# Layer 1's heads: three row blocks of the first head come early into the unused third pair of split weights, gated rows leave from the normed tile

## The chip, the core and the metric

The kernel runs on one core of one Trainium2 chip. The core has five engines that run at the same time, each through its own list of instructions in order: PE (matrix products; PEld is its weight load), DVE and ACT (elementwise work), POOL (here small elementwise work and the issue of some DMAs) and SP (the issue of most DMAs). An instruction waits at the head of its engine's list until the semaphores it needs are set, and everything behind it on that engine waits with it. The metric is the device time of one launch in microseconds (us); lower is better.

## The reference, cut to what matters

Two layers work on a prompt of 512 tokens and on 8 running streams of 16 new tokens, 640 rows together, with a width of 2048. Layer 0 is an attention layer and is not touched here. Layer 1 is gated linear attention with 4 heads, keys of 256 and values of 512 per head:

```python
def gla_chunk(S, inp):
    q, k, v, g = inp
    b = jnp.cumsum(g, axis=1)
    ...
    o = jnp.einsum('bhcs,bshe->bche', a, v) + jnp.einsum('bchd,bhde->bche', q_in, S)
    S = jnp.exp(b_last)[..., None] * S + jnp.einsum('bshd,bshe->bhde', k * jnp.exp(b_last[:, None] - b), v)
    return S, o

def gla_mixer(h, w_in, w_a2, b_a, g_out, w_out, S0=None):
    ...
    q, k, v, r, a_lr = jnp.split(h @ w_in, [nk, 2 * nk, 2 * nk + nv, 2 * nk + 2 * nv], axis=-1)
    ...
    o = o * lax.rsqrt(jnp.mean(o * o, axis=-1, keepdims=True) + EPS) * g_out...
    y = (o.reshape(B, T, nv) * jax.nn.silu(r.astype(f32))) @ w_out
```

So each head's output rows are normed, multiplied by a gate, and then go through the output weights w_out (2048 by 2048). In the trunk the product is gated again, added to the residual, and normed once more.

## The kernel before, in words

**Precision.** Every large product is made of three products of rounded halves. A helper `halves(hi, lo, x)` (L133) copies x into hi on ACT (L134) and puts x minus hi into lo on DVE (L135). `split` (L139) does so for a raw weight tile of 128 by 1024. It takes one of two pairs of tiles (tags wh and wl in the pool wp), and every third time, where `ring3["pool"]` is set, a third pair in another pool. Raw weights come through two tiles (tag wr).

**Order.** PE's list is written out by hand. As the code writes it, it keeps a clock of its own, `pe["now"]` (L50), to which each product adds its estimated time (L54 to L63: a product of 512 columns adds 512/2400 + 0.0133). The main work is a generator that is driven step by step. After each step `Side.tick` (L316) looks at the lanes, which are generators of side work, and lets those run whose due time on this clock has come; `side.after(wait, what)` (L288) puts a call at a time. `side.until(condition)` (L335) does side work only: where nothing is due it moves the clock by 0.2 and tries again. Waits written in the code (`yield step(5.0)`) are thus places in PE's list and not times on the chip. The lists of the other four engines are ordered by a scheduler that looks ahead over the whole program.

**The stage.** In the last part of layer 1, the main work is first `plain` (L629): 24 pieces of q and k weights, each with 48 products of 320 columns (L651). Pieces 22 and 23 make the last 128 columns; piece 22 reads the tiles in the slots 16 to 31 of `hp`, piece 23 those in the slots 0 to 15. Then come two calls of `share` (L683): share g multiplies head g's four row blocks of gated output (each 128 by 640) by the head's rows of w_out, in four column stretches c and five token blocks a. One step of it is three products of 512 columns (L697) for one row block, and the first token block goes through the row blocks 0, 1, 2, 3 in turn.

**Side work in this stage.** `decays` (L1601) makes q and k of a head ready. `prompt_lane` (L1662) goes through 16 units (head, chunk of 128 tokens). For each it makes the output `o`, norms it into a tile `on` (two buffers, L1567 to L1576), and one unit later calls `leave` (L1589): four transposes of `on` on PE (L1593), the product with the gate tile on DVE, written over the gate tile (L1594), and a DMA on POOL's queue that takes the gate tile to a DRAM tensor `og_d` (L1595). The next gate tile is fetched by `fetch_gate`, also on POOL's queue (L1580). `sample_lane` (L1791) does the same for the running streams. For each head it takes 32 state tiles of 128 by 512 (tag s0, seven buffers, S0 = 7 on L34; numbers below count them over all heads), in groups of four: `ask` (L1775) loads one, a product reads it (L1855), PE and DVE update it (L1861, L1863), and `leaves` (L1786) stores it to the output 1.0 later on the clock and asks for another one 7.0 after that. With seven buffers, state n + 7 can only be asked for when state n has left. All these loads and stores are on POOL's queue. The product of L1855 may be put into the list in the very step in which its last state is asked for.

**Row blocks.** The lane `fetches` (L1878) brings back the row blocks from `og_d` through two tiles (tag pl), which `plain` also uses for its results (L1504), and splits each into two slots of `hp`. It starts with block 0 when half of piece 23 is placed (`came["last"]`, L1505), waits 5.0, asks for blocks 0 and 1, waits 4.0, splits 0, and then goes on 0.5 apart. The first share begins when four blocks are split and 2.0 have passed:

```python
                side.until(lambda: came["rows"] >= 4 * g + 4 and pe["now"] > came["at"] + 2.0)
                drive(share(g, og1, w_out1, first=first))
```

The raw weights of the first share's two pieces are asked for before that, and the third pair of split weights (pool w4, 2 tiles of 128 by 1024) is opened after `plain`. Memory for it is there all through the stage.

Of the kernel before, what the change touches and what calls it, by code (L numbers as in the profile page):

```python
# [8 lines left out]
F32 = mybir.dt.float32  # L9
# [4 lines left out]
ALU = mybir.AluOpType  # L14

P = 128
# [5 lines left out]
T = NP + NB * NT  # L22
# [19 lines left out]
def hybrid_step_kernel(ctx: ExitStack, tc: tile.TileContext, A: dict, O: list):  # L42
# [4 lines left out]
    dve = nc.vector  # L47


    pe = {"now": 0.0, "quad": 4800}  # L50
# [19 lines left out]
    def load(out, in_):  # L70
        nc.sync.dma_start(out=out, in_=in_)
# [4 lines left out]
    def move(out, in_):  # L76

        nc.gpsimd.dma_start(out=out, in_=in_)
# [42 lines left out]
    og_d = [dp.tile([P, 4, T], F32, name=f"og_{h}") for h in range(GH)]  # L121
# [11 lines left out]
    def halves(hi, lo, x, e=None):  # L133
        nc.scalar.copy(hi, x)  # L134
        (e or dve).tensor_tensor(lo, x, hi.bitcast(F32), op=ALU.subtract)  # L135

    ring3 = {"n": 0, "pool": None, "tags": ("wh", "wl")}

    def split(x):  # L139

        n = ring3["n"] = ring3["n"] + 1
        third = ring3["pool"] is not None and n % 3 == 0
        h, lo = ((ring3["pool"] if third else wp).tile([P, 1024], F32R, tag=t, name=t[:2], bufs=1 if third else 2)
                 for t in (ring3["tags"] if third else ("wh", "wl")))
        h, lo = (t[:, :x.free_size()] for t in (h, lo))
        halves(h, lo, x)
        return h, lo

    def wraw(src, a, n):
        r = wp.tile([P, 1024], F32, tag="wr", name="wr", bufs=WR)[:, :a * n]  # L150
        load(r.rearrange("p (a n) -> p a n", a=a), src)
        return r
# [113 lines left out]
    def slot(n, shape=(P, T), dt=F32R, name="h"):  # L266
        return hp.tile(list(shape), dt, tag=f"t{n}", name=name)
# [6 lines left out]
    def step(wait=0.0, tp=0, z=0, tiled=False):  # L274
        return wait, tp, z, tiled

    class Side:
# [14 lines left out]
        def share(self, **bufs):  # L292
            self.free = {k: [0.0] * n for k, n in bufs.items()}
# [5 lines left out]
        def next(self, lane):  # L299
            what = next(lane[0], None)  # L300
            if what is None:
                self.lanes.remove(lane)
            else:
                lane[1] = (pe["now"] + what[0], {"tp": what[1], "z": what[2]}, what[3])
# [39 lines left out]
    side = Side()  # L344

    def drive(*gens):
        for g in gens:
            for _ in g:
                side.tick()
# [330 lines left out]

    y_t = {}

    def share(g, og, w, leave=None, at=None, first=None):  # L683


        src = w.rearrange("(kt p) n -> p kt n", p=P)

        def raw(c, i):
            return wraw(src[:, 4 * g + 2 * i:4 * g + 2 * i + 2, 512 * c:512 * c + 512], 2, 512)

        def products(acc, a, i, w):
            wh, wl = w
            for e in range(2):
                kt = 4 * g + 2 * i + e
                h, lo = (x[:, P * a:P * a + P] for x in og[kt])
                for l, r, first, last in ((h, wh, True, False), (h, wl, False, False), (lo, wh, False, True)):
                    mm(acc, l, by(l, r[:, e, :]), start=i == 0 and e == 0 and first, stop=i == 1 and e == 1 and last)  # L697
                yield

        def add(a, c, pt):  # L700
            if g:
                dve.tensor_tensor(y_t[a, c], pt, y_t[a, c], op=ALU.add)  # L702
            else:
                y_t[a, c] = slot(5 * c + a, (P, 512), F32, "y")
                nc.scalar.copy(y_t[a, c], pt)

        leave = leave or add
        raws = list(first or [raw(0, 0), raw(0, 1)])

        def made():  # L710
            return [t.rearrange("p (a n) -> p a n", a=2) for t in split(raws.pop(0))]

        w0, w1 = made(), made()
        for c in range(4):
            ws = [w0, w1]
            if c < 3:
                raws += [raw(c + 1, 0), raw(c + 1, 1)]
            if at:
                at(c)
            each = (0, 1, 2) if leave is add or c < 3 else (4, 1, 2, 3, 0)  # L720
            for a in each:
                acc = bank("mm")
                for i in range(2):
                    yield from products(acc, a, i, ws[i])
                leave(a, c, acc)
                if a == each[0] and c < 3:
                    w0 = made()
            if len(each) == 3:
                acc = {a: bank("mm") for a in (3, 4)}
                for i in range(2):  # L730
                    for a in (3, 4):
                        yield from products(acc[a], a, i, ws[i])
                        if i:
                            leave(a, c, acc[a])
                    if i == 0 and c < 3:
                        w1 = made()
# [16 lines left out]
    with tc.tile_pool(name="st", bufs=1, reuse_waits="tile") as st:  # L753
# [21 lines left out]
        for a in range(TOK):  # L775
            ss4 = st.tile([P, 4], F32, tag="ss4", name="ss4", bufs=2)
            for q in range(4):
# [3 lines left out]
                tp = bank("mm")  # L781
# [8 lines left out]
            if a == 2:  # L790
                tp = bank("tp")
# [118 lines left out]
    with tc.tile_pool(name="kp", bufs=2, reuse_waits="tile") as kp, \  # L910
# [47 lines left out]
        pairs, since, through, z_t = {}, {}, {"p0": 0, "p1": 0, "s": 0}, {}  # L958
# [258 lines left out]
        first = [wraw(w_out0.rearrange("(kt p) n -> p kt n", p=P)[:, n:n + 2, :512], 2, 512) for n in (12, 14)]  # L1217
# [10 lines left out]
    with tc.tile_pool(name="o0", bufs=1, reuse_waits="tile") as po, ExitStack() as only_d:  # L1228
# [3 lines left out]
        t = sp.tile([P, 1280], F32, tag="s2", name="c1")  # L1232
# [3 lines left out]
        t = sp.tile([P, 512], F32R, tag="s7", name="middles")  # L1236
# [147 lines left out]
        r = wp.tile([P, 1024], F32, tag="wr", name="wr", bufs=WR)[:, :256].rearrange("p (k n) -> p k n", k=KT)  # L1384
# [73 lines left out]
        n = 0  # L1458
# [30 lines left out]
    og1 = {}  # L1489

    def w_of(g, c, i):

        k0 = 4 * g + 2 * i
        return w_out1.rearrange("(kt p) n -> p kt n", p=P)[:, k0:k0 + 2, 512 * c:512 * c + 512]

    with tc.tile_pool(name="gl", bufs=1, reuse_waits="tile") as gl:
        came = {"plain": False, "last": False, "of": 0, "when": 0.0}

        def keep(dst, hh):
            t = []  # L1500

            def leave(nt, pt):
# [4 lines left out]
                if nt:  # L1507
                    nc.scalar.dma_start(out=dst[:, hh, :], in_=t[0])
                    for h in range(1, GH):
                        if hh and dst is gk_d[h]:  # L1510
# [3 lines left out]

        others = plain(h2, src, [(n0 + P * hh, keep(dst, hh)) for h in range(1, GH)
                                 for n0, dst in ((256 * h, gq_d[h]), (NK + 256 * h, gk_d[h])) for hh in range(2)],
                       lambda: came.update(plain=True))
        for _ in range(2):
            next(others)

# [68 lines left out]
        def leave(h, t0, on, g):  # L1589

            tp = bank("tp")
            for s in range(4):
                turn_block(tp[:, P * s:P * s + P], block(on[:, P * s:P * s + P]), ident)  # L1593
            dve.tensor_tensor(g, tp.rearrange("p (s t) -> p s t", s=4), g, op=ALU.mult)  # L1594
            move(og_d[h][:, :, t0:t0 + P], g)  # L1595


        ready, through = {}, {"p": 0, "s": 0}
# [192 lines left out]
        def sample_lane():  # L1791
# [11 lines left out]
            for h in range(GH):  # L1803
# [70 lines left out]
                if h + 1 < GH:  # L1874
                    yield step(4.0)
                    here = fetch(h + 1)

        def fetches():  # L1878

            def free(kt):  # L1880
                g, s = kt // 4, kt % 4
                return came["plain"] and came["shares"] >= min(2, g if s > 1 else g - 1)

            rows = {}

            def ask_rows(kt):
                rows[kt] = gl.tile([P, T], F32, tag="pl", name="og_in", bufs=2)
                load(rows[kt], og_d[kt // 4][:, kt % 4, :])

            for kt in range(10):  # L1890
                while min(through.values()) <= kt // 4 or not came["last"]:
                    yield step(0.5)
                if kt not in rows:
                    yield step(5.0)
                    ask_rows(kt)
                    if kt % 4 < 3 and kt < 9 and came["plain"]:
                        ask_rows(kt + 1)
                    yield step(4.0)
                while not free(kt):
                    yield step(0.3)  # L1900
                n = 20 + 2 * kt % 12
                og1[kt] = slot(n, name="ogh"), slot(n + 1, name="ogl")
                halves(*og1[kt], rows.pop(kt))
                if kt % 4 < 3 and kt < 9 and kt + 1 not in rows:
                    ask_rows(kt + 1)
                came["rows"], came["at"] = kt + 1, pe["now"]
                yield step(0.5)
# [2 lines left out]
        for x in (decays(), prompt_lane(), sample_lane(), fetches()):  # L1910
            side.add(x)
        drive(others)
        with tc.tile_pool(name="w4", bufs=1, reuse_waits="tile") as w4:
            ring3["pool"] = w4
            first = [wraw(w_of(0, 0, i), 2, 512) for i in range(2)]
            for g in range(2):
                side.until(lambda: came["rows"] >= 4 * g + 4 and pe["now"] > came["at"] + 2.0)
                drive(share(g, og1, w_out1, first=first))
                came["shares"] = g + 1
                first = [wraw(w_of(g + 1, 0, i), 2, 512) for i in range(2)]  # L1920
            ring3["pool"] = None
            parts = [split(r) for r in first]
            first = [wraw(w_of(3, 0, i), 2, 512) for i in range(2)]
            side.finish()


    share_banks(mm=8)
# [96 lines left out]
```

## Time and profile before

| what | value |
|---|---|
| time, median of 3 runs | 2552.77 us |
| the three runs | 2552.77, 2548.27, 2553.05 us |
| the profiled execution, whole | 2548.99 us |
| its span in the trace | 2547.3 us |
| DVE, ACT, POOL busy in the span | 1581.5, 995.4, 162.4 us |
| HBM traffic over the span | 196 GB/s |
| the stage of layer 1's heads | about 1990 to 2427 us in the span |

The page gives one profiled execution. Its span runs from the first instruction to the last; the whole execution is 1.7 us longer. A view by stretches gives the busy time of each engine between two times, and TensorE's granted clock. The view of the timeline lists instructions with their start, their duration, the engine, the line, the tiles written and read, and in brackets how long the engine had been idle before and what released it; "SPq" and "ACTq" are the issue of a DMA, not its transfer. The view of waits sums for each pair who waited for whom: us in total, times, the longest. Releasers are inferred, and a wait for several things is put down to the one that came last.

### The profile page before, as it was taken

How to read it: one execution, taken by the hardware profiler on the slowest of the kernel's cores; microseconds unless marked ns; L12 is line 12 of the kernel's file. 1: busy time of each engine (PE TensorE's matmuls, PEld its weight loads, DVE VectorE, ACT ScalarE, POOL GpSimd, SP SyncE). 2: the span in 40 equal slices, each digit the busy share in tenths (PEclk: the TensorE clock that was granted, in tenths of full speed). 3: DMA queues.
4: the chain of work that ended last, by engine and by line, in shares of the span. 5: the costliest groups of instructions: out<-in, count | busy, mean ns of one | idle time of the engine just before them, and what ended most of it. 6: DMA issues, size and time to landing. Idle time of an engine off the chain costs nothing.

```text
span 2547.3 us, 43980 instructions
## 1 busy us (share of the span) xinstructions
PE 2438.0 (96%) x17561; PEld 2156.7 (85%) x17561; DVE 1581.5 (62%) x2565; ACT 995.4 (39%) x1730; POOL 162.4 (6%) x390
## 2 busy tenths in 40 slices
PE   7899999999999999999999989999999999979998
PEld 5589999999999989788887768999999988857776
DVE  5675655556566656666775677566767465555456
ACT  4332222222223335555452454333333454455223
POOL 0010000000000000000000000000000233243100
PEclk8899999999999999999999989999999999989999
DMA  9966666666663367788864754344444777785634
GB/s 344 330 212 223 208 206 214 229 215 214 202 201 116 120 198 223 249 247 264 258 206 124 233 168 124 95 127 134 117 115 118 211 231 242 231 284 192 211 119 146
DMA packets 469439, 503.13 MB, mean 198 GB/s; under 512 B 42730, under 2 KB 366450, under 8 KB 469106
## 3 DMA queue, kind: packets, MB, share of 16 engines
q1 hardware_dynamic: 446274, 436.60, 54.6%
q0 software_dynamic: 16048, 51.92, 6.1%
q10 hardware_dynamic: 6912, 11.80, 1.2%
q8 instruction: 138, 2.26, 0.4%
q14 instruction: 67, 0.55, 0.1%
HBM read 411.10 MB, written 89.13 MB: 196 GB/s over the span
## 4 chain that ended last, share of the span: by engine, by line
PE 74%; DMA 7%; DVE 5%; ACT 3%; issue 3%; POOL 1%; ACTq 0%; SPq 0%; POOLq 0%; DVEq 0%
PE ps_mm L592 38%; PE ps_mm L697 11%; PE ps_mm L651 6%; PE ps_mm L367 3%; PE ps_tp L1080 2%; DMA gv<-kr 2%; PE ps_tp L1132 1%; PE ps_mm L516 1%; PE ps_tp L1040 1%; PE ps_z L1016 1%; PE ps_z L180 1%; PE ps_tp L1546 1%; PE ps_z L1094 1%; ACT wh L134 1%; PE ps_z L222 1%
## 5 line engine op out<-in xcount | busy, mean ns | idle before, releaser
L592 PE MATMUL ps_mm<-sums,wh 128*128 128x320 f32 x2752 | 615.7, 312 | 3.8 <-ACT wh L134 3.8
L592 PEld LDWEIGHTS ps_mm<-sums,wh 128*128 128x128 f32 x2752 | 459.7, 189 | 12.9 <-issue 7.0
L592 PE MATMUL ps_mm<-h,wh 128*128 128x320 f32 x2064 | 461.8, 312 | 4.8 <-DVE u L598 4.8
L592 PE MATMUL ps_mm<-sums,wl 128*128 128x320 f32 x1376 | 426.7, 310 | 1.4 <-DVE wl L135 1.4
L135 DVE TENSOR_TENSOR wl<-wr,wh 128x1024 fp32r<-128x1024 f32 x194 | 237.3, 1224 | 243.9 <-ACT wh L134 238.2
L592 PEld LDWEIGHTS ps_mm<-h,wh 128*128 128x128 f32 x2064 | 343.1, 188 | 20.8 <-issue 12.1
L134 ACT CAST wh<-wb 128x1024 fp32r<-128x1024 f32 x170 | 178.4, 1050 | 428.1 <-PE ps_mm L592 357.3
L134 ACT CAST wh<-wr 128x1024 fp32r<-128x1024 f32 x194 | 203.7, 1050 | 351.0 <-PE ps_mm L592 185.6
L592 PE MATMUL ps_mm<-h,wl 128*128 128x320 f32 x1032 | 318.8, 309 | 0.0
L651 PE MATMUL ps_mm<-h,wh 128*128 128x320 f32 x1152 | 268.7, 320 | 8.9 <-ACT wh L134 4.4
L592 PEld LDWEIGHTS ps_mm<-sums,wl 128*128 128x128 f32 x1376 | 259.4, 189 | 1.9 <-DVE wl L135 1.9
L135 DVE TENSOR_TENSOR wl<-wb,wh 128x1024 fp32r<-128x1024 f32 x170 | 207.9, 1223 | 63.7 <-ACT wh L134 63.2
L651 PEld LDWEIGHTS ps_mm<-h,wh 128*128 128x128 f32 x1152 | 195.9, 192 | 25.5 <-issue 12.3
L697 PE MATMUL ps_mm<-wh,ogh 128*128 128x512 f32 x460 | 201.4, 438 | 4.7 <-DVE y L702 3.5
L592 PEld LDWEIGHTS ps_mm<-h,wl 128*128 128x128 f32 x1032 | 193.7, 188 | 0.0
L697 PE MATMUL ps_mm<-wh,ogl 128*128 128x512 f32 x460 | 181.2, 394 | 0.3 <-DVE ogl L135 0.3
L697 PE MATMUL ps_mm<-wl,ogh 128*128 128x512 f32 x460 | 181.3, 394 | 0.0
L651 PE MATMUL ps_mm<-h,wl 128*128 128x320 f32 x576 | 180.4, 313 | 0.7 <-DVE wl L135 0.7
L697 PEld LDWEIGHTS ps_mm<-wh,ogh 128*128 128x128 f32 x460 | 87.2, 189 | 33.4 <-issue 18.2
L651 PEld LDWEIGHTS ps_mm<-h,wl 128*128 128x128 f32 x576 | 110.4, 192 | 1.0 <-DVE wl L135 1.0
L697 PEld LDWEIGHTS ps_mm<-wh,ogl 128*128 128x128 f32 x460 | 86.8, 189 | 20.7 <-DVE ogl L135 0.7
L697 PEld LDWEIGHTS ps_mm<-wl,ogh 128*128 128x128 f32 x460 | 87.5, 190 | 11.2 <-issue 0.2
(357 smaller groups left out, 3733.7 us busy)
## 6 DMA issues: line engine op xcount, KB each, us to landing
ar<-in_w_ada_dram SPq DMA_DIRECT2D x160, 512.0 KB
wb<-in_sb_w_in_dram SPq DMA_DIRECT2D x82, 512.0 KB
kc<-in_cache_sb_k_dram SPq DMA_DIRECT2D x64, 512.0 KB
vc<-in_cache_sb_v_dram SPq DMA_DIRECT2D x64, 512.0 KB
wr<-in_gla_w_in_dram SPq DMA_DIRECT2D x51, 512.0 KB
wb<-in_gla_w_in_dram SPq DMA_DIRECT2D x45, 512.0 KB
wr<-in_sb_w_in_dram SPq DMA_DIRECT2D x44, 512.0 KB
ar<-in_w_ada_dram SPq DMA_DIRECT2D x64, 256.0 KB
```

The costliest lines, as they stand in the source:

```text
L134: nc.scalar.copy(hi, x)
L135: (e or dve).tensor_tensor(lo, x, hi.bitcast(F32), op=ALU.subtract)
L180: mm(acc[32 * q:32 * q + 32, :w], cT[:, kt + m, :], by(cT[:, kt + m, :], rs[m // each][:, m % each, q, :]), start=kt + m == 0, stop=kt + m ...
L222: mm(acc[32 * j:32 * j + 32, :256], cT[:, kt + m, :], by(cT[:, kt + m, :], r[:, 256 * j:256 * j + 256]), start=kt + m == 0, stop=kt + m == ...
L367: mm(acc[a], l[:, c], by(l[:, c], r[:, k2, :]), start=kt == k0 and first, stop=kt == k0 + nk - 1 and last)
L516: mm(acc[a], l, by(l, r[:, e, :]), start=j == 0 and e == 0 and begun, stop=j == 7 and e == 1 and last)
L592: mm(acc, l[:, k, :], by(l[:, k, :], r), start=start and k == 0 and first, stop=k == 7 and last, skip_group_check=True)
L651: mm(acc[nt], l[:, k, :], by(l[:, k, :], r), start=k0 == 8 and k == 0 and first, stop=k0 == 0 and k == 7 and last)
L697: mm(acc, l, by(l, r[:, e, :]), start=i == 0 and e == 0 and first, stop=i == 1 and e == 1 and last)
L1016: mm(z[:, :n], q[:, hh, qs], by(q[:, hh, qs], k[:, hh, :n]), start=True, stop=True)
L1040: mm(o[:, :P], l, by(l, aT[:, kb, :]), start=kb == 0, stop=kb == qb)
L1080: turn_block(tp[:, P * c:P * c + P], block(kc[:, c, P * hh:P * hh + P]), ident)
```

## The change

The pool w4 is opened at the start of the stage. When the first head has left in both lanes, and 8.0 later, its row blocks 0, 1 and 2 are loaded into w4's two tiles: 1024 columns hold one block of 640 and 384 columns more, so block 2 lies in both. They are split as soon as piece 22 of `plain` is placed. Block 3 is asked for when half of piece 23 is placed, without the wait of 5.0. The first share is begun in the middle: its raw weights are asked for and its first piece is split after piece 22 of `plain`, the second piece when the share goes on, after four blocks are split and 2.0 have passed, as before. And the gated rows are written into the normed tile `on`, which the DMA then stores, and no longer into the gate tile.

```diff
-    def share(g, og, w, leave=None, at=None, first=None):
+    def share(g, og, w, leave=None, at=None, first=None, apart=False):
...
-        w0, w1 = made(), made()
+        w0 = made()
+        if apart:
+            yield
+        w1 = made()
...
-    with tc.tile_pool(name="gl", bufs=1, reuse_waits="tile") as gl:
+    with tc.tile_pool(name="gl", bufs=1, reuse_waits="tile") as gl, \
+            tc.tile_pool(name="w4", bufs=1, reuse_waits="tile") as w4:
...
-                       lambda: came.update(plain=True))
+                       lambda: upper())
...
-            dve.tensor_tensor(g, tp.rearrange("p (s t) -> p s t", s=4), g, op=ALU.mult)
-            move(og_d[h][:, :, t0:t0 + P], g)
+            on = on.rearrange("p (s t) -> p s t", s=4)
+            dve.tensor_tensor(on, tp.rearrange("p (s t) -> p s t", s=4), g, op=ALU.mult)
+            move(og_d[h][:, :, t0:t0 + P], on)
...
+        def upper():
+            came.update(plain=True)
+            begun.append(share(0, og1, w_out1, first=[wraw(w_of(0, 0, i), 2, 512) for i in range(2)], apart=True))
+            next(begun[0])
+
+        def row(kt):
+            n = 20 + 2 * kt % 12
+            og1[kt] = slot(n, name="ogh"), slot(n + 1, name="ogl")
+            return og1[kt]
+
         def fetches():
...
+            while min(through.values()) < 1:
+                yield step(0.5)
+            yield step(8.0)
+            x = [w4.tile([P, 1024], F32, tag=t, name="og_in") for t in ("wh", "wl")]
+            for n in range(2):
+                load(x[n][:, :T], og_d[0][:, n, :])
+            load(x[0][:, T:], og_d[0][:, 2, :1024 - T])
+            load(x[1][:, T:2 * T - 384], og_d[0][:, 2, 1024 - T:])
+            while not came["plain"]:
+                yield step(0.3)
+            for kt in range(2):
+                halves(*row(kt), x[kt][:, :T])
+                yield step(0.8)
+            to = row(2)
+            halves(*[t[:, :1024 - T] for t in to], x[0][:, T:])
+            halves(*[t[:, 1024 - T:] for t in to], x[1][:, T:2 * T - 384])
+            came["rows"], came["at"] = 3, pe["now"]
...
-            for kt in range(10):
+            for kt in range(3, 10):
                 while min(through.values()) <= kt // 4 or not came["last"]:
-                    yield step(0.5)
+                    yield step(0.3)
                 if kt not in rows:
-                    yield step(5.0)
+                    if kt > 3:
+                        yield step(5.0)
                     ask_rows(kt)
-                    if kt % 4 < 3 and kt < 9 and came["plain"]:
+                    if 3 < kt < 9 and kt % 4 < 3:
                         ask_rows(kt + 1)
                     yield step(4.0)
...
-        with tc.tile_pool(name="w4", bufs=1, reuse_waits="tile") as w4:
-            ring3["pool"] = w4
-            first = [wraw(w_of(0, 0, i), 2, 512) for i in range(2)]
-            for g in range(2):
-                side.until(lambda: came["rows"] >= 4 * g + 4 and pe["now"] > came["at"] + 2.0)
-                drive(share(g, og1, w_out1, first=first))
...
+        for g in range(2):
+            side.until(lambda: came["rows"] >= 4 * g + 4 and pe["now"] > came["at"] + 2.0)
+            ring3["pool"] = w4
+            drive(share(g, og1, w_out1, first=first) if g else begun[0])
```

More of the change, by code (lines that the diff above doesn't have):

```diff
@@ L1876, in sample_lane @@
                     here = fetch(h + 1)
+        begun = []
+        def upper():
[6 more added lines that the diff above has]
+            return og1[kt]
         def fetches():
@@ L1881, in free @@
                 g, s = kt // 4, kt % 4
-                return came["plain"] and came["shares"] >= min(2, g if s > 1 else g - 1)
+                return came["shares"] >= min(2, g if s > 1 else g - 1)
+            while min(through.values()) < 1:
[15 more added lines that the diff above has]
+            came["rows"], came["at"] = 3, pe["now"]
             rows = {}
@@ L1900, in fetches @@
                     yield step(0.3)
-                n = 20 + 2 * kt % 12
-                og1[kt] = slot(n, name="ogh"), slot(n + 1, name="ogl")
-                halves(*og1[kt], rows.pop(kt))
+                halves(*row(kt), rows.pop(kt))
                 if kt % 4 < 3 and kt < 9 and kt + 1 not in rows:
@@ L1912, in hybrid_step_kernel @@
         drive(others)
-        with tc.tile_pool(name="w4", bufs=1, reuse_waits="tile") as w4:
+        for g in range(2):
+            side.until(lambda: came["rows"] >= 4 * g + 4 and pe["now"] > came["at"] + 2.0)
             ring3["pool"] = w4
-            first = [wraw(w_of(0, 0, i), 2, 512) for i in range(2)]
-            for g in range(2):
-                side.until(lambda: came["rows"] >= 4 * g + 4 and pe["now"] > came["at"] + 2.0)
-                drive(share(g, og1, w_out1, first=first))
[L1919 to L1924, printed above, removed]
+            drive(share(g, og1, w_out1, first=first) if g else begun[0])
+            came["shares"] = g + 1
+            first = [wraw(w_of(g + 1, 0, i), 2, 512) for i in range(2)]
+        ring3["pool"] = None
+        parts = [split(r) for r in first]
+        first = [wraw(w_of(3, 0, i), 2, 512) for i in range(2)]
+        side.finish()
     share_banks(mm=8)
```

## The prediction

> **What bounds the kernel now.** First the page's head: PE is busy nearly throughout, so time can be won only where PE stands still or is slowed.
>
> ```profile
> span 2547.3 us, 43980 instructions
> PE 2438.0 (96%) x17561; PEld 2156.7 (85%) x17561; DVE 1581.5 (62%) x2565; ACT 995.4 (39%) x1730; POOL 162.4 (6%) x390
> ```
>
> Next, where it stands still: the view by stretches around the change (columns: length, busy time per engine, granted clock, DMA share, GB/s).
>
> ```profile
> core 0: us, PE busy (x) PEld busy (x) DVE busy (x) ACT busy (x) POOL busy (x), PEclk, DMA share, GB/s
> 2108.00:2130.00 22.00, 22.00 (x145) 21.15 (x146) 9.02 (x20) 10.14 (x21) 6.61 (x11) 1.00 0.97 275
> 2130.00:2188.00 58.00, 52.13 (x330) 45.19 (x330) 33.61 (x55) 25.62 (x48) 21.07 (x35) 0.97 0.75 242
> 2215.00:2257.00 42.00, 42.00 (x263) 36.05 (x262) 26.09 (x45) 20.98 (x42) 12.75 (x23) 1.00 0.69 227
> 2257.00:2280.00 23.00, 7.08 (x23) 2.35 (x21) 14.19 (x24) 11.87 (x20) 8.98 (x15) 0.77 0.95 323
> 2280.00:2375.00 95.00, 94.36 (x446) 73.74 (x446) 55.45 (x94) 51.86 (x95) 32.07 (x55) 0.98 0.62 206
> ```
>
> From 2257 to 2280, between `plain` and the first share, PE does 7.08 us of work in 23: 15.92 us are idle. Behind it PE is full, so work brought into this gap shortens the run. The timeline of PE there:
>
> ```profile
> 2257.08 0.85 PE L1861 MATMUL ps_tp<-vst,kst 128*128 128x512 f32 x3
> 2261.58 0.40 PE L697 MATMUL ps_mm<-wh,ogh 128*128 128x512 f32 x1
> 2262.38 1.79 PE L1855 MATMUL ps_z<-s,qz 128*32 128x512 f32 x6
> 2278.26 1.91 PE L1855 MATMUL ps_z<-s,qz 128*32 128x512 f32 x2 [14.09 <-DMA s<-in_state_gla_dram]
> ```
>
> One step of the share is done, then the list holds the states' product (L1855) of head 2's last group, whose fourth state (number 47) comes only at 2278.2: 14.09 us. The row blocks are the second lock on the same gap; SP's issue of the first, second and third, DVE's split of the fourth, and, for later use, the weight cast that piece 22 released:
>
> ```profile
> 2247.74 0.38 SPq L71 DMA_DIRECT2D og_in<-og  x1
> 2257.10 0.32 SPq L71 DMA_DIRECT2D og_in<-og  x1
> 2264.70 0.32 SPq L71 DMA_DIRECT2D og_in<-og  x1
> 2276.95 0.83 DVE L135 TENSOR_TENSOR ogl<-og_in,ogh 128x640 fp32r<-128x640 f32 x1 [0.61 <-ACT ogh L134]
> 2243.41 1.05 ACT L134 CAST wh<-wr 128x1024 fp32r<-128x1024 f32 x1 [0.27 <-PE ps_mm L651]
> ```
>
> The fourth is ready at 2277.8, half a microsecond before the state. So removing either lock alone wins nearly nothing. The change removes the rows' lock; the question is what it does to the states' one.
>
> **The change part by part.** *Rows 0 to 2.* Their three loads and three splits move, and block 2 becomes two loads and four smaller split operations. The splits stay off the path: ACT is idle half of 2215 to 2257 (20.98 of 42), and they can start when piece 22 releases its slots, about 2243 as that cast shows. Block 3 is asked for as soon as block 0 was, 2247.74, and its split should end where block 0's did, about 2257.1, when `plain` ends. The share's second weight split must now wait for the rows to leave w4; any delay of it, or of block 3, up to the remaining stall costs nothing, because PE would stand at L1855 anyway.
>
> *What PE does before the state's product.* Here the list's order decides. From the point `came["last"]` the code counted 5.0 + 4.0 + 3 x 0.5 + 2.0 = 12.5 on its own clock until the share; now it counts 4.0 + 2.0 = 6.0, so the share begins 6.5 earlier in the list. State 47 does not move: it is asked for 1.0 + 7.0 behind the first L1861 of the group before, which follows `plain` as it did. One step of the share moves the clock by 3 x (512/2400 + 0.0133) = 0.68, which makes 9.6 steps; the transposes (L1593) and the two L1630 that the idle clock held now take some of that, so I count 7 more steps before L1855 (6 to 9). What one costs:
>
> ```profile
> 2372.27 5.51 PE ps_mm L697 x24
> ```
>
> 5.51 / 24 x 3 = 0.69 us a step. Seven steps are 4.8 us (4.1 to 6.2). If the state lands at the same time, PE comes to it some 3 us later, does 4.8 us more and stalls about 11 us instead of 14: gain 4.8.
>
> *When state 47 lands.* POOL's timeline, from the store that frees its buffer to its load:
>
> ```profile
> 2263.39 0.60 POOL L78 DMA_DIRECT2D out_dram<-s  x1 [0.42 <-issue]
> 2266.52 1.09 POOL L78 DMA_DIRECT2D out_dram<-s  x2 [1.59 <-DVE ogl L135]
> 2271.62 0.72 POOL L78 DMA_DIRECT2D og<-gate  x1 [3.01 <-issue]
> 2274.14 0.56 POOL L78 DMA_DIRECT2D s<-in_state_gla_dram  x1 [1.80 <-issue]
> out_dram<-s POOLq DMA_DIRECT2D x16, 256.0 KB, 5.5
> 2274.14 4.07 DMA s<-in_state_gla_dram
> ```
>
> The store lands after 5.5 us, at 2268.9; the load goes 5.2 us later, behind other work of the queue, and lands in 4.1 us. None of that is removed by the diff, so 0 is one end and 5.2 us the other; the load can also come later if the queue's order turns out worse, which I bound by the largest issue gap here, 3.0 us. What leaves this stretch is traffic: rows 1 and 2 are 2 x 128 x 640 x 4 = 0.66 MB, at the stretch's 323 GB/s 2.0 us. I take 1.5 us, nearest to that row.
>
> *Gate stores.* A gate load waited until the store of the gate tile had landed; now it waits only for DVE.
>
> ```profile
> L78 POOL DMA_DIRECT2D og<-gate x20: 719/737/764, 2061.9 to 2373.6; - x20
>   POOL gate L78: 19.6, 8
> 2180.74 0.78 POOL L78 DMA_DIRECT2D gate<-gr  x1 [1.20 <-DMA og<-gate]
> 2182.03 0.55 POOL L78 DMA_DIRECT2D s<-in_state_gla_dram  x1
> 2187.52 1.92 PE L1855 MATMUL ps_z<-s,qz 128*32 128x512 f32 x2 [5.87 <-DMA s<-in_state_gla_dram]
> ```
>
> That is 19.6 us of POOL's queue in 8 waits, but POOL is no bound; only one of them, 1.20 us, stands right before a load that PE then waits for (5.87 us, head 1's last group). I take 1.0 us (0 to 1.2).
>
> *The price of `on`.* The normed tile is now held until its store has landed. It has two buffers, so a unit's norm waits for the store of the unit before the last. The tightest place and the landing times (min, median, max):
>
> ```profile
> 2245.16 0.74 POOL L78 DMA_DIRECT2D og<-gate  x1 [0.64 <-DVE gate L1594]
> 2252.10 0.60 ACT L1571 ACTIVATE on<-ps_tp 128x512 f32<-128x512 f32 x1 [1.16 <-PE ps_tp L1546]
> DMA to landing us min/median/max: 2.5/4.7/8.2
> ```
>
> 6.9 us between issue and reuse against 4.7: 2.2 us to spare. I take 0; at the largest landing it is 1.3 us on ACT.
>
> *Early traffic.* The first head's last rows leave here:
>
> ```profile
> 2119.45 0.73 POOL L78 DMA_DIRECT2D og<-gate  x1 [1.05 <-DVE on_ms L232]
> ```
>
> So 0.98 MB moves to about 2119 to 2130, where the DMA share is 0.97 at 275 GB/s: 3.6 us of transfer. SP may also stand until those last rows have landed, 4.7 us. PE was full in that stretch and the weights are split one piece ahead, so I take 0, up to 3.6 us if all of it delays a state. The Trainium skill, "DMA: Bandwidth & Descriptors", section "Issuing engines are not separate DMA queues", speaks against the change here: DMAs from SP and POOL run on the same 16 engines and interleave, so SP's early rows would take time from POOL's states. By that alone the sum would be 3.6 us worse; the trace agrees that the engines are full there (0.97), but shows no PE wait in those 22 us.
>
> Sum: 4.8 + 1.5 + 1.0 = 7.3 us. The profiled execution, 2548.99 us with its 1.7 us around the span, would become 2541.7. The median shown, 2552.77, lies 3.8 above that execution, and the three runs spread over 4.8; the same sum from the median is **2545.5 us**.
>
> **The rivals.** *The state's lock goes too.* If state 47 lands 5 us earlier and the full count of 9 steps fits, the stall shrinks to some 4 us, and with the 1.2: 6.2 + 5.2 + 1.2 = 12.6, so 2540.2. For it: 3.0 and 1.8 us of POOL's gaps have no cause that the profile names, and one gap of 1.59 us ends with a split of a row block on DVE, which will no longer be there. Against: the store's 5.5 us and the load's 4.1 us stay. The Trainium skill, "SBUF — State Buffer", section "SBUF: two separate sides", gives a reason for such gaps: DVE and GpSimd share one port pair, and POOL cannot write its descriptors while DVE holds it; the row of 1.59 us agrees with it, no row here proves it. Chance 0.13.
>
> *Given back at the end of the second share.* It now runs some 7 us ahead of the sample lane, whose last gated rows SP awaits before it fetches the next weights:
>
> ```profile
> 2371.47 8.16 SPq L71 DMA_DIRECT2D og_in<-og  x6
> 2381.15 0.40 SPq L71 DMA_DIRECT2D wr<-in_gla_w_out_dram  x1
> 2393.08 1.05 ACT L134 CAST wh<-wr 128x1024 fp32r<-128x1024 f32 x1 [7.40 <-PE ps_mm L697]
> ```
>
> If the six row loads stay ahead of the weights at 2381.15, these are split at 2391 or later while PE wants them 7 us before 2393: up to 5 us come back, leaving 2.3, so 2550.5. Against: the weights are now free to go 7 us earlier, ahead of rows that cannot come yet, and the scheduler orders SP's list by what is ready. Likewise state 47 may land up to 3 us later. Chance 0.20.
>
> *Slower, through `on`.* Besides the place shown, two more have little room between store and reuse:
>
> ```profile
> 2076.84 0.73 POOL L78 DMA_DIRECT2D og<-gate  x1 [0.29 <-issue]
> 2084.60 0.57 ACT L1571 ACTIVATE on<-ps_tp 128x512 f32<-128x512 f32 x1
> 2339.75 0.76 POOL L78 DMA_DIRECT2D og<-gate  x1
> 2347.26 0.60 ACT L1571 ACTIVATE on<-ps_tp 128x512 f32<-128x512 f32 x1
> ```
>
> That is 7.8 and 7.5 us. If the POOL queue adds its 3.0 us gap to the longest landing, 11.2 us, ACT stands 4.3 + 3.4 + 3.7 = 11.4 us before a norm, with the weight casts behind it, and the PSUM bank held. It decides from a landing of 6.9 us, costs PE only where a cast is late by a piece, and at its full price, with the gain at its lower end (4.1), gives 7.3 us slower: 2560. Chance 0.09.
>
> *The change doesn't do what it says.* SP's loads are put into its list so late that the rows come as before, or block 3 alone holds the share until 2277: 2552. Chance 0.05.
>
> **How the numbers follow.** The forecast (a gain of 4.8 to 9) has 0.53. A measurement of this kernel can tell about 0.2%, 5.1 us, from no change. Faster by more: the first rival and most of the forecast, 0.13 + 0.47 = 0.60. Within: the low end of the forecast, the giving back and the change without effect, 0.06 + 0.20 + 0.05 = 0.31. Slower: 0.09. The range reaches from the first rival, counted from a run near the lower end of those shown (2548.27 - 12.6 = 2535.7; I take 2537), to no gain at the highest run, 2553.
>
> **What would show it.** Right: rows 0 to 2 loaded between 2119 and 2135 and split near 2245; the first product of the share within 2 us of `plain`'s end; 8 steps (6 to 10) of L697 before the L1855 of head 2's last group, and still a wait of 5 to 11 us there with the slow 1.9 us product behind it; no POOL wait of a gate load for its store; no ACT wait of L1571 for a store. Wrong: L1855 without a wait (first rival), a wait of L697 for weights behind SP's row loads near 2385 (second), ACT L1571 released by the rows' store (third), or row loads of block 0 still at 2247.

## The result, and the profile after

The changed kernel is slower.

| | before | after |
|---|---|---|
| time, median (range) of 6 runs each, one chip | 2552.19 us (2547.3 to 2554.33) | 2579.48 us (2572.24 to 2585.78) |
| ratio after to before, 95% interval | | 1.0113, 1.0096 to 1.0131 |
| span of the profiled execution | 2547.3 us | 2576.5 us |

The forecast was 2545.5 us, with 0.09 for slower. In the changed kernel the lines of the states and norms lie 3 to 5 lower: L1855 is now L1860, L1861 L1866, L1571 L1575, L1593 L1597, L1594 L1599; the code is the same except where the diff shows it. (In the runs 1 and 12 L1855 is L1859, in run 2 L1856.)

The page's head of the kernel after. The matrix products are the same 17561, yet PE is busy 8.9 us longer:

```profile
span 2576.5 us, 44013 instructions
PE 2446.9 (95%) x17561; PEld 2158.5 (84%) x17561; DVE 1582.1 (61%) x2566; ACT 994.4 (39%) x1731; POOL 164.1 (6%) x390
```

Where in the span? The view by stretches for PE alone, over the stage, from the last product of the stage before it to the first product of the one behind it (columns: stretch, length, PE busy, granted clock, DMA share, GB/s). First the kernel before, then the one after:

```profile
1988.60:2433.40 444.80, 412.26 (x2326) 0.98 0.72 228
```

```profile
1985.50:2462.60 477.10, 426.74 (x2325) 0.94 0.68 213
```

The stage takes 32.3 us more. In 14.5 of them PE is busy longer with the same products, at a clock that is lower on average; in 17.8 it is idle. Over the stage the engines of the DMA moved fewer bytes per second than before. What PE waits for is the first line of its view of waits in this stage (whom for whom: us, times, longest), before and after:

```profile
PE ps_z L1855 <- DMA s<-in_state_gla_dram: 20.9, 3, 14.1
```

```profile
PE ps_z L1860 <- DMA s<-in_state_gla_dram: 38.8, 7, 13.7
```

The states come late, in seven places instead of three, and behind most of these waits the products run slowly for a while (1.91 us for two products of L1860, which take 1.04 behind a short wait; rows of both stand below). So the question is why the states are loaded late. POOL issues their loads. From POOL's view of waits, the lines in which POOL stood ahead of a DMA and no semaphore explains it ("issue"), and the one line in which a gate load waited for the store; first before:

```profile
POOL s L78 <- issue: 23.7, 17, 3.8
POOL gate L78 <- DMA og<-gate: 19.6, 8, 5.0
POOL gate L78 <- issue: 12.2, 7, 5.5
POOL og L78 <- issue: 4.2, 4, 3.0
POOL out_dram L78 <- issue: 3.1, 6, 1.4
```

And after:

```profile
POOL gate L78 <- issue: 73.6, 18, 6.2
POOL out_dram L78 <- issue: 12.5, 4, 6.6
POOL s L78 <- issue: 6.3, 6, 3.7
POOL og L78 <- issue: 5.7, 5, 3.6
POOL vst L78 <- issue: 0.5, 1, 0.5
```

The wait for the store's semaphore is gone, as the change intends, and in its place POOL stands 73.6 us ahead of the gate loads with no semaphore to name. Added up, the lines with "issue" are 43.2 us before and 98.6 after. This sum is called POOL's **issue idle** below, always from 1960 to 2480 us.

One place in detail: POOL's timeline around the first such wait of PE, before:

```profile
2088.56 0.75 POOL L78 DMA_DIRECT2D og<-gate  x1 [0.21 <-issue]
2089.27 0.58 POOL L78 DMA_DIRECT2D out_dram<-s  x1
2092.72 0.55 POOL L78 DMA_DIRECT2D s<-in_state_gla_dram  x1 [2.87 <-DMA out_dram<-s]
2093.36 0.54 POOL L78 DMA_DIRECT2D out_dram<-s  x1
2094.03 0.73 POOL L78 DMA_DIRECT2D out_dram<-S  x1
2094.75 0.57 POOL L78 DMA_DIRECT2D out_dram<-s  x1
2098.13 0.77 POOL L78 DMA_DIRECT2D gate<-gr  x1 [2.81 <-issue]
```

And after, with the product that waits:

```profile
2090.23 0.74 POOL L78 DMA_DIRECT2D og<-on  x1
2096.45 0.79 POOL L78 DMA_DIRECT2D gate<-gr  x1 [5.47 <-issue]
2097.22 0.55 POOL L78 DMA_DIRECT2D out_dram<-s  x1
2097.76 0.55 POOL L78 DMA_DIRECT2D s<-in_state_gla_dram  x1
2104.37 1.91 PE L1860 MATMUL ps_z<-s,qz 128*32 128x512 f32 x2 [6.99 <-DMA s<-in_state_gla_dram]
```

Before, the scheduler knew that the gate load had to wait for the store of the rows to land, and put the states' DMAs between the two. Now the gate load has nothing to wait for, so it stands directly behind the store: in 17 of the 20 places of POOL's list, where it was 1 before. But it is not issued there. POOL stands for 5.5 us, and the store and the load of the state, which need no gate, stand behind it. Near the end of that time the engines of the DMA have almost nothing to move, so it is not for them that POOL waits (changed kernel; columns: stretch, length, POOL busy, PE's clock, DMA share, GB/s):

```profile
2093.80:2095.70 1.90, 0.00 (x0) 1.00 0.11 35
```

The store of rows issued at 2090.23 landed 5.8 us later, at about 2096.0, and the gate load follows at 2096.45.

### The profile page after: what moved, and what is told of

Its sections match the earlier page's. It is cut to its first block, busy times and chain, and to the rows that moved or that the text cites. A ratio compares the mean times of both kernels' runs of the same rounds, so it can differ in the third digit from the quotient of the medians.

```text
span 2576.5 us, 44013 instructions
## 1 busy us (share of the span) xinstructions
PE 2446.9 (95%) x17561; PEld 2158.5 (84%) x17561; DVE 1582.1 (61%) x2566; ACT 994.4 (39%) x1731; POOL 164.1 (6%) x390
## 5 line engine op out<-in xcount | busy, mean ns | idle before, releaser
L697 PE MATMUL ps_mm<-wh,ogh 128*128 128x512 f32 x460 | 202.7, 441 | 4.2 <-DVE y L702 3.5
L697 PE MATMUL ps_mm<-wh,ogl 128*128 128x512 f32 x460 | 182.3, 396 | 0.3 <-DVE ogl L135 0.3
L697 PE MATMUL ps_mm<-wl,ogh 128*128 128x512 f32 x460 | 182.2, 396 | 0.0
L697 PEld LDWEIGHTS ps_mm<-wh,ogh 128*128 128x128 f32 x460 | 87.9, 191 | 34.3 <-issue 19.3
L697 PEld LDWEIGHTS ps_mm<-wh,ogl 128*128 128x128 f32 x460 | 87.3, 190 | 20.9 <-DVE ogl L135 0.7
L697 PEld LDWEIGHTS ps_mm<-wl,ogh 128*128 128x128 f32 x460 | 88.2, 192 | 11.3 <-issue 0.2
```

## The experiments

Three theories. **P**: what costs is POOL's list, as just described. **O**: the normed tile is held until its store has landed, and ACT, PSUM and PE are late by that. **R**: the early row blocks do it, by their traffic or their place. P came to have two forms, P1 (POOL stands because there is no room for more descriptors of its DMAs) and P2 (it stands for another reason). The room is a number in `kernel()`, `dynamic_dma_scratch_size=1024`: the bytes of each partition that the program sets aside for the descriptors of POOL's DMAs.

The ratio is to the kernel before on the same chip. "Waits" are those of PE for state loads.

| | kernel | median, us | ratio (95%) | issue idle, us | waits, us (times) |
|---|---|---|---|---|---|
| 1 | early rows alone | 2546.53 | 1.0001 (0.9986 to 1.0016) | 37.0 | 15.5 (4) |
| 2 | leave from `on` alone | 2576.46 | 1.0117 (1.009 to 1.0144) | 98.6 | 36.9 (6) |
| 3 | after, 1088 bytes | 2575.02 | 1.0118 (1.0095 to 1.0141) | 62.6 | 36.9 (7) |
| 4 | after, gate loads on SP | 2542.87 | 0.9986 (0.9972 to 0.9999) | 28.0 | 15.3 (5) |
| 5 | after, 1728 bytes | 2553.35 | 1.0014 (0.9998 to 1.003) | 10.6 | 16.4 (5) |
| 6 | before, 1728 bytes | 2549.34 | 0.9997 (0.9982 to 1.0012) | 5.7 | 19.2 (3) |
| 7 | after, gates in runs of 2 KB | 2552.6 | 1.0011 (0.9995 to 1.0028) | 36.1 | 19.2 (5) |
| 8 | as 4, traced once more | 2543.08 | one run | 20.1 | 14.4 (5) |
| 9 | after, 1408 bytes | 2555.67 | 1.0031 (1.0015 to 1.0048) | 31.9 | 19.4 (6) |
| 10 | early rows alone, gate loads on SP | 2549.98 | 1.0003 (0.9991 to 1.0015) | 16.6 | 15.4 (4) |
| 11 | as 4, 1728 bytes | 2549.13 | 1.0003 (0.9989 to 1.0016) | 10.6 | 13.3 (4) |
| 12 | as 1, more runs | 2546.77 | 0.9988 (0.9973 to 1.0003) | 50.3 | 18.7 (4) |

The median before was 2548.13 us beside 1 to 4, 2549.54 beside 5 to 8, and 2547.57 beside 9 to 12.

One part of the issue idle is no lack of room. In the runs 4, 7, 8 and 11 it holds a gap of 8.3 to 8.4 us ahead of the last store of rows of the stage. The same gap is there in the changed kernel and in the runs 3, 5 and 9 (8.26 to 8.38), where the view names what ends it, DVE's product L1599.

**1 and 2: which half of the change?** The first is the changed kernel with the old leave, the second the kernel before with the new one:

```diff
# 1, against after
-            on = on.rearrange("p (s t) -> p s t", s=4)
-            dve.tensor_tensor(on, tp.rearrange("p (s t) -> p s t", s=4), g, op=ALU.mult)
-            move(og_d[h][:, :, t0:t0 + P], on)
+            dve.tensor_tensor(g, tp.rearrange("p (s t) -> p s t", s=4), g, op=ALU.mult)
+            move(og_d[h][:, :, t0:t0 + P], g)
```

> Only the early rows, the opened share and the split: the gated rows again leave from the gate tile. Theory P (POOL's list: the gate load now stands right behind the store of the gated rows, and the later of the two holds POOL for 3 to 6 us, so that the state loads behind it are asked late): 2545 us, within 4, as the product with S1's states has its old list; waits of PE for states no more than 21 us in 3 or 4. Theory O (the normed tile is held until its store has landed): the same. Theory R (the early loads of rows and their splits push the state loads back): 2570 to 2580, with some 39 us of waits for states in 7.

> Only the other half: the kernel before, with the gated rows leaving from the normed tile. Theories P and O: 2570 to 2590 us, slower than before by 18 to 38, with waits of PE for states of over 30 us. Theory R: 2552 within 4, as before.

The leave alone costs 28.3 us at the medians, as much as the whole change; the rows alone cost nothing. R falls. The second kernel's two lines, from the views of waits of PE and of POOL, are those of the changed kernel over again:

```profile
PE ps_z L1856 <- DMA s<-in_state_gla_dram: 36.9, 6, 19.4
POOL gate L78 <- issue: 72.1, 18, 6.0
```

**4: the gate load out of POOL's list.**

```diff
# against after
-            move(g, gr_d[h][:, :, t0:t0 + P])
+            load(g, gr_d[h][:, :, t0:t0 + P])
```

> The changed kernel with the 20 gate loads on SP's queue in place of POOL's. Theory P in both forms: POOL's list holds no gate load, the state loads behind are asked in time, 2540 to 2553 us, unless SP's queue is late for the early rows. Theories O and R: 2579 within 6.

> One more look at the changed kernel with its gate loads on SP's queue, for its trace: theory O (the normed tile is held until its store has landed) would have ACT or PE wait for the store, over 10 us in all; the other theories under 5.

The second text belongs to the eighth row of the table, the same kernel run once more. All the loss is gone with the leave from `on` kept, so O falls too. ACT's view of waits says the same: in neither of these two runs, nor in the changed kernel, does a norm (L1575) wait for a store of rows. What it waits for most is PE's product with the states. Of the changed kernel, then of run 8:

```profile
ACT on L1575 <- PE ps_z L1860: 34.5, 4, 10.8
```

```profile
ACT on L1575 <- PE ps_z L1860: 13.4, 4, 10.2
```

**3, 5 and 9: more room for descriptors.** The only edit is that number, in the changed kernel: 1088, 1728, 1408.

> The changed kernel, with 1088 bytes per partition for the descriptors of POOL's DMAs in place of 1024. Theory P in its narrow form (two DMAs of 512 pieces need 66 descriptors of each of 16 rings, and 64 fit, so that the second of the pair waits until the first has been worked off): POOL's idle time ahead of the gate loads falls from 73.6 us in 18 to under 15, waits of PE for states to 21 or less, time 2540 to 2553. Theory P in its wide form (any two such DMAs within a few us collide, whatever the memory): 2579 within 6 and 73 us as in the changed kernel. Theories O and R: 2579 within 6, with or without the idle time.

> The changed kernel with 1728 bytes per partition for the descriptors of POOL's DMAs (1024 in the changed kernel, 1088 in the third experiment, where the idle time ahead of the gate loads fell from 73.6 to 42.2 us and the time stayed). Theory P1 (POOL stands because the descriptors of the DMAs before have not been worked off, the states' among them): the idle time ahead of the gate loads under 15 us, waits of PE for states 21 or less, 2538 to 2553 us. Theory P2 (POOL stands for another reason, and what costs is that the gate load with its 512 pieces goes ahead of the states' pieces on the same 16 engines): the idle time may fall, the time stays within 6 of 2577.

> The changed kernel with 1408 bytes for POOL's descriptors, between the sizes tried (idle time of POOL put down to issue, all of its DMAs, from 1960 to 2480 us: 98.6 us at 1024 bytes, 62.6 at 1088, 10.6 at 1728; time 2579, 2575, 2553). Theory P1 with a count of 33 descriptors for a DMA of 512 pieces and 9 for a state's: 88 fit, which is the pair and two states: idle time 15 to 35 us, time 2553 to 2562. If the time goes with the idle time in a line between the known ends, 2556 to 2565; if the gate load had only to fit beside one store of rows, under 15 us and 2553.

With 1728 bytes POOL's list is as in the changed kernel, the gate load directly behind the store of rows, and POOL no longer stands. The timeline of the same place:

```profile
2092.11 0.74 POOL L78 DMA_DIRECT2D og<-on  x1
2092.86 0.80 POOL L78 DMA_DIRECT2D gate<-gr  x1
2093.64 0.55 POOL L78 DMA_DIRECT2D out_dram<-s  x1
2096.27 0.55 POOL L78 DMA_DIRECT2D s<-in_state_gla_dram  x1 [2.08 <-DMA out_dram<-s]
```

The load goes out 0.75 us behind the store instead of 6.22, and the state's load now waits only for the store that frees its tile: it goes out 4.16 us behind the store of rows, as in the kernel before, where it was 7.53 in the changed one. The time falls from 1.0113 to 1.0014 of before; at 2553.35 us it is 0.35 above the range expected of P1, and far from the 2577 of P2. This is P1: the same list, the same transfers, only more room. The sizes between show how it goes: 98.6, 62.6, 31.9 and 10.6 us of issue idle give ratios of 1.0113, 1.0118, 1.0031 and 1.0014. It is no straight line: the first third of the idle time that was taken away, at 1088, won nothing that the times show, and the run fits neither form of P in its own expectation. PE there waited for states in seven places, as in the changed kernel, four of the waits of 4.86 to 14.59 us, and POOL still stood up to 4.5 us ahead of single gate loads. (In the one trace of each, the stage is 8.0 us shorter than in the changed kernel, 469.1 and 477.1; the four times of this kernel don't confirm it.) Why just those states stayed late is open.

The narrow form of P1 in the third expectation came from the Trainium skill, "DMA: Bandwidth & Descriptors": its section "SWDGE vs HWDGE vs iDMA" says that GpSimd writes the descriptors of its own DMAs into rings kept in SBUF, its section "Terms" gives 16 bytes for one, and "The descriptor swizzle" counts, for a transfer to 128 partitions, 8 on each engine for the pieces and one for the completion. An estimate from this page: 1024 bytes hold 64; a DMA of 512 pieces takes 33 on each of 16 engines; the store of rows and the gate load together take 66. By that estimate 68, the room of 1088 bytes, would have been enough, and the run says that it was not: 42.2 us ahead of gate loads remained. The states' DMAs are in flight as well, and take their part; 1408 bytes took most of it, 1728 nearly all. That POOL stands while there is no room is read from the traces.

**6: the same room before.** A control:

> The kernel before with the same 1728 bytes: a control. Theory P1: the gate loads there wait by a semaphore until the store has landed, so there is little to gain: 2541 to 2550 us, at most 5 below before. Theory P2: the same as before within 3.

```profile
POOL s L78 <- issue: 2.1, 4, 1.4
POOL s L78 <- DMA out_dram<-s: 44.3, 28, 4.8
POOL gate L78 <- DMA og<-gate: 30.5, 11, 4.4
POOL gate L78 <- issue: 1.1, 2, 0.7
```

43.2 us of issue idle fall to 5.7 and the time does not move. So the idle time of POOL without a named cause was a lack of room in the kernel before too. Most of it comes back under a name: the gate loads wait 10.9 us more for the store of the gate tile (19.6 before), and the loads of states 16.7 us more for the store that frees their tile (27.6 before). With room POOL comes earlier to waits that it has anyway. The idle time was on show in the prediction's own rows (3.01 and 1.80 us in brackets before state 47), as a gain for the first rival.

**7: fewer pieces.** The gates are kept in DRAM so that a gate load is 128 runs of 2 KB and not 512 of 512 bytes.

```diff
# against after
-    gr_d = [dp.tile([P, 4, T], F32, name=f"gr_{h}") for h in range(GH)]
+    gr_d = [dp.tile([P, TOK, 4, P], F32, name=f"gr_{h}") for h in range(GH)]
...
-            move(g, gr_d[h][:, :, t0:t0 + P])
+            move(g, gr_d[h][:, t0 // P, :, :])
```

> The changed kernel with the gates kept in DRAM as 128 runs of 2 KB for each block of 128 tokens, so that a gate load is 128 pieces in place of 512; it stands at the same place of POOL's list. Theory P1: a load of few pieces finds room at once; idle time ahead of gate loads under 15 us, 2540 to 2555 us. Theory P2: if the number of pieces is what delays the states, the same gain, but with the idle time left; if the place in the list alone, 2577 within 6.

The third way to the same end. POOL's idle time ahead of gate loads falls to 3.0 us in 6 and the loss goes. The issue idle is 36.1 us in all, 16.1 of it ahead of stores of rows; half of these is the gap of 8.4 us named below the table, and the other 7.7 may have moved there from the gate loads. It costs little there.

**10 and 11: what is the leave from `on` worth without the harm?** 10 is 1 with the gate loads on SP's queue, 11 is 4 with 1728 bytes.

> Early rows alone (gated rows leave from the gate tile), gate loads on SP's queue: each gate load now waits in SP's list for the store of the rows to land, with the loads of weights behind it. The theory that the leave from the normed tile helps once POOL is out of the way: 3 to 10 us slower than the fourth experiment (2543), so 2546 to 2553. The theory that it is worth nothing, as POOL and SP have room: 2543 within 3.

> The changed kernel with the gate loads on SP's queue and 1728 bytes for POOL's descriptors. Theory P1: the fourth experiment leaves POOL some 25 us of issue idle ahead of loads and stores of states; if they lie on the path, 2538 to 2541; if they are covered, 2543 within 2.

Not settled to the microsecond. 4 and 10 differ in the direction expected (0.9986 and 1.0003, some 4.3 us by these ratios), though their intervals overlap, and in 10 SP waits 77.1 us in 16 places for the store of a gate tile to land, where it is 15.2 us in 3 in run 1. But 11, which has less idle time than 4, came out at 1.0003, above both of its forecasts, so the differences among these are near what can be told apart. No version here beats the kernel before by more than 0.2%; the best is 4, by 0.14%, with an interval that ends at 0.9999.

**12: what are the early rows worth?**

> The first experiment once more, with more rounds, to bound the worth of the early rows. The sum of the prediction for this part: 0.9975 of before (6.3 us). Rival: the state's product is asked earlier and waits as much longer, the rest is given back: 0.9990 to 1.0005.

0.9988, and 1.0001 in the first: between the forecast's 0.9975 and nothing; the forecast lies just inside the one interval and outside the other. The traces show where some of a gain may go. PE's timeline of the first experiment, at the wait that the prediction was about and at the last states of the stage:

```profile
2255.44 0.40 PE L697 MATMUL ps_mm<-wh,ogh 128*128 128x512 f32 x1
2262.52 1.06 PE L1859 MATMUL ps_z<-s,qz 128*32 128x512 f32 x6
2272.25 1.92 PE L1859 MATMUL ps_z<-s,qz 128*32 128x512 f32 x2 [8.67 <-DMA s<-in_state_gla_dram]
2360.43 1.04 PE L1859 MATMUL ps_z<-s,qz 128*32 128x512 f32 x2 [2.56 <-DMA s<-in_state_gla_dram]
```

The first share begins with the end of `plain`, nine of its steps come before the states' product (27 products of L697), and the wait is 8.67 us where it was 14.09. In the last line is a wait that the kernel before does not have. PE by stretches (columns as above), before and then the first experiment:

```profile
2255.00:2345.00 90.00, 73.44 (x338) 0.92 0.67 217
2345.00:2425.00 80.00, 77.87 (x348) 1.00 0.61 208
```

```profile
2255.00:2345.00 90.00, 81.14 (x377) 0.94 0.65 218
2345.00:2425.00 80.00, 73.95 (x312) 0.96 0.59 197
```

In the first stretch PE does 39 products more; in the second 36 fewer, at a clock of 0.96 instead of 1.00. (Run 6, without the early rows, has 361 and 354, so part of such a difference lies between any two executions.) The twelfth run shows the same waits: 9.70 us instead of 14.09 at the first place, and 2.57 us at the last. The reason may be that the sample lane's last states come by their own chain of stores and loads, which is no earlier because PE is ahead; this was not tested. The stage as a whole, measured as above, takes 444.8 us before and 444.3 in run 6, and 440.8 and 446.7 in the runs 1 and 12: no gain that these runs agree on.

## Why the prediction was wrong

**The step that failed is "Gate stores".** It read "a gate load waited until the store of the gate tile had landed; now it waits only for DVE", and took 1.0 us of gain, bounded by 0 and 1.2, with the 19.6 us in 8 waits as a thing that could only go. Two things were missing. The wait was also what kept the two DMAs apart in the scheduler's list, so taking it away moved 17 gate loads up to stand right behind a store of rows. And POOL has no room for the descriptors of both beside those of the states: 73.6 us of standing in place of 19.6. The measured price of this half is 28.3 us (the second experiment), not a gain of 1.0. The bound was made from the row of one wait on the path, and not from the question of what would stand there next.

**"POOL is no bound" was not enough.** By its busy time it was not, 6% before and after. But its list carries the states' loads, for which PE waits, and idle time of POOL with no cause was in the prediction's own rows. It had 43.2 us of it, which the sixth run showed to be lack of room, and the longest gap was 5.5 us, where the prediction reckoned with 3.0 at most. There was no gain in these gaps of the kind that the first rival hoped for: with the gaps gone in run 5, PE still waits 8.54 us for state 47, and 8.67 in run 1, which has them. The reason given for such gaps by the first rival, that DVE holds the port (the Trainium skill, "SBUF — State Buffer", "SBUF: two separate sides"), is not what made most of them: more room for descriptors, with DVE's work unchanged, took 43.2 us to 5.7. In the kernel before this idle time cost nothing that can be measured, as run 6 shows; in the changed kernel it came to stand ahead of the states.

**"Rows 0 to 2", "Early traffic": right.** SP issues three of the four loads at 2131.12 us in the changed kernel, the forecast being 2119 to 2135; the fourth, the 192 KB of block 2 that were stored first, went out ahead of that, at 2096.09. In the first experiment they are split from 2237 on (forecast: near 2245), and the first share begins within 2 us of the end of `plain` in both. The rows alone cost nothing measurable.

**"What PE does before the state's product": right.** Seven more steps than the one of before were counted, 8 in all (6 to 10), with 5 to 11 us of wait left; it is nine steps in the changed kernel and in the runs 1 and 12, and 8.67 and 9.70 us in these two. In the changed kernel the wait stays at 13.67 us in spite of the nine steps, because the state comes late: its product starts 21.8 us behind the first product of the share, where it is 16.8 in run 1.

**The gain of the rows: too large.** Of 4.8 + 1.5 us the measurement without the other half, runs 1 and 12, shows between none and about 3. What these two traces have in common with the rival "given back at the end of the second share" is a new wait late in the stage, 2.56 and 2.57 us; it is for the last states and not for weights behind SP's row loads, which the rival named. That this wait is what took the gain is not shown.

**"The price of `on`": right at 0.** No wait of a norm for a store of rows was found in the changed kernel, nor in runs 4 and 8. The rival "slower, through `on`" thus had the right sign and part of the change, and the wrong mechanism.

What the sum would have been with the one term mended is to be seen in 4: the change with its gate loads out of POOL's list, 0.9986.

## What to carry to other kernels

When a change takes a wait away, ask what a scheduler will do with the instruction that is now free, and who is behind it in its new place: on a queue issued in order, an instruction that can be listed early but not yet issued holds all that follows. Idle time ahead of POOL's DMAs that no semaphore explains can be a sign that room for descriptors is short, as most of it was here; it is cheap to try with a larger number, with DMAs of fewer and longer pieces, or with another issuing queue. And a gain at a wait in the middle of a stage is a gain only if the chain that ends the stage comes earlier too.

## What the runs showed of the hardware

- POOL stands ahead of its next DMA when there is no room for its descriptors, also while the engines of the DMA are nearly idle (share 0.11 for 1.9 us). In the changed kernel this idle time in the stage was 98.6 us at 1024 bytes per partition, 62.6 at 1088, 31.9 at 1408 and 10.6 at 1728; it appears in the profile as "issue" and is not in POOL's busy time.
- The number of pieces counts, not the bytes alone: the gate load of 256 KB in 512 pieces had 73.6 us of idle time ahead of it over the stage, in 128 pieces 3.0.
- A wait of some microseconds costs PE more than its length. The fourteen traces hold 68 waits of PE for a state. Behind each of the 20 of up to 1.28 us the granted clock over the next 6 us was 1.00; behind each of the 39 of 2.56 us or more it was 0.75 or less; the nine of 1.56 to 2.28 us show both. Of the 32.3 us that the stage grew by, 14.5 are the same products taking longer, at a clock of 0.94 on average instead of 0.98. An estimate from the rows of the clock (busy time times what the clock lacks to 1.00, in stretches of 5 us) puts some 10 of them down to the clock.
